# Row sums of the later modulation: transposed 32x32 blocks on VectorE instead of 512-column products on TensorE

## Chip, core and metric

The kernel runs on one core of a Trainium2 chip. The metric is the device time of one execution in microseconds (us). TensorE is PE in the profile (PEld are its weight loads), VectorE is DVE, ScalarE ACT, GpSimd POOL, and SyncE's transfer queue SPq.

## What is computed

A decoder trunk of two layers over 512 positions of width 2048: first differential attention, then forgetting attention on keys and values that are projected once from the stream after the first layer. Each layer shifts, scales and gates its input by vectors that come from one conditioning row c:

```python
c_act = silu(c)                                   # (1, 2048)
mod = c_act @ w_mod[l] + b_mod[l]                 # (1, 3 * 2048): shift, scale, gate
h = x * (1.0 + scale[:, None]) + shift[:, None]
y = mixer(h)                                      # attention of the layer
x = layer_norm(DN_ALPHA * x + gate[:, None] * y, ln_g[l], ln_b[l])
```

The shared keys and values have a shift and a scale of their own (`kv_w_mod`, `kv_b_mod`). So there are eight vectors of 2048 values, each a product of one row with a 2048x2048 matrix. The shift and scale of layer 0 are needed before anything else; this case is about the other six: gate of layer 0, shift and scale of the shared keys and values, shift, scale and gate of layer 1.

## The kernel before, in words

**The large products.** All weights come in as f32, two row blocks of 128 at a time (`WeightStream`, lines 50 to 106; tile wst), and are split into a rounded half whi (ScalarE, L93) and a remainder wlo (VectorE, L94). `group` (lines 306 to 348) runs one job of 512 columns: for each pair of row blocks and each of four accumulator banks a burst of six products, `products` (L173, L174, L175): high by high, high by low, low by high. After every burst it calls `tick`.

**What goes on beside them.** `tick` (line 290) takes the next entry of `pieces`, a list written out by hand with the steps of attention (score, turn, values, norm, store), and then advances the generator `background` as often as its argument bg says. The order in which the instructions of an engine end up is not only that of the code: a scheduler of the framework orders them by priority and readiness, so that ready work can stand earlier on its engine than the loop issues it. Between engines, waits follow from the tiles: a tile with bufs=1 can be written again only when its last reader is done.

**The later modulation.** `mod_stream` (lines 355 to 399) is that background. It works through segments of 512 columns. For each segment it loads the matrix's 16 row blocks (tile ms, or msk) and adds them up on VectorE, each row weighted by its value of c_act: one `tensor_scalar` (L389) and 15 `scalar_tensor_tensor` (L391) of 128x512 into the accumulator macc (two buffers). One tick is one of these 16 instructions. What is left is the sum over the 128 partitions. `mod_row` (lines 401 to 415) makes it, in two steps that run within the next segment, at its second and its sixth tick: first macc is split into mhi (ScalarE) and mlo (VectorE) by `split` (L168, L169; one buffer each) and the bias is loaded into mrow (L408); then two products with a 128x128 matrix of ones, 512 columns wide (L411, L412), give the row sum in the bank tr, VectorE adds the bias (L413, one partition, 512 values), and the row is stored to DRAM (L414).

There are two such streams. The first (lines 630 to 649) has four vectors, 16 segments: `gate_dram[0]`, both rows of `mod_dram[0]`, and the first row of `mod_dram[1]`. Its first tick is issued in the group qk[3], behind the first three heads' work; qk groups advance it in two bursts of three, vg groups in three of four, and what is left runs in `open_n` (line 913). The attention steps of heads 0 and 1 stand close together in `pieces`; from head 2 on they are spread out (`spread=True`). The second stream (lines 1090 to 1105) has two vectors, 8 segments (the second row of `mod_dram[1]` and `gate_dram[1]`), beside the projection of the shared values and keys (vj, kj). `fold` (line 931) reads `mod_dram[0]` back in `open_n` and `mod_dram[1]` during kj[2]; the gates are read in `out_projection` (line 884).

The bank tr (`tr_bank`, one buffer) is shared by these products and all transpositions on PE. Weights, ms, biases and rows all are issued in order on SyncE's queue.

Of the kernel before, what the change touches and what calls it, by code (L numbers as in the profile page):

```python
# [2 lines left out]

# [6 lines left out]
F32 = mybir.dt.float32  # L10
F32R = mybir.dt.float32r
I32 = mybir.dt.int32
AF = mybir.ActivationFunctionType
ALU = mybir.AluOpType

P = 128
D = 2048
# [92 lines left out]
def tile_yoco(  # L110
# [23 lines left out]
    nc = tc.nc  # L134
    V, S, PE, G = nc.vector, nc.scalar, nc.tensor, nc.gpsimd
# [6 lines left out]
    const = ctx.enter_context(tc.tile_pool(name="const", bufs=1))  # L142
# [12 lines left out]
    def acc_bank(name="acc"):  # L155
        return ps.tile([P, 512], F32, name=name, tag="acc", bufs=4)
# [4 lines left out]
    def tr_bank(name="tr"):  # L161
        return ps.tile([P, 512], F32, name=name, tag="tr", bufs=1)
# [4 lines left out]
    def split(hi, lo, src):  # L167
        S.copy(hi, src)  # L168
        V.tensor_tensor(lo, src, hi.bitcast(F32), op=ALU.subtract)  # L169
# [8 lines left out]
    ident = const.tile([P, P], F32, name="ident")  # L178
    make_identity(nc, ident)
    ones = const.tile([P, P], F32, name="ones")  # L180
    G.memset(ones, 1.0)
    mask = const.tile([P, 512], F32, name="mask")
    G.memset(mask, 0.0)
    G.affine_select(
# [14 lines left out]
    pt = tr_bank()  # L199
# [7 lines left out]
    pt = tr_bank()  # L207
# [147 lines left out]
    def mod_stream(segs, new_stage, new_acc, nk, deep=0, new_deep=None):  # L355

        todo = [(i, r) for i in range(len(segs)) for r in range(KT // nk)]
        loaded = {}  # L360
        summed = []

        def load(k):
            i, r = todo[k]
            src, col, _ = segs[i]
            t = new_deep() if k < deep else new_stage()
            rows = src[nk * r * P : nk * (r + 1) * P, col : col + 512]
            nc.sync.dma_start(t, rows.rearrange("(k p) n -> p k n", p=P) if nk > 1 else rows)
            loaded[k] = t

        def load_upto(k):
            n = len(loads)
            while n < len(todo) and n <= (k + 7 if n < deep else k + 2 // nk):
                load(n)
                loads.append(n)
                n += 1

        loads = []
        load_upto(-1)
        for k, (i, r) in enumerate(todo):  # L380
            load_upto(k)
            if r == 0:
                acc = new_acc()
            t = loaded.pop(k)
            for kk in range(nk):
                kt = nk * r + kk
                w = t[:, kk, :] if nk > 1 else t
                if kt == 0:
                    V.tensor_scalar(acc, w, cact[:, 0:1], None, op0=ALU.mult)  # L389
                else:  # L390
                    V.scalar_tensor_tensor(acc, w, cact[:, kt : kt + 1], acc, op0=ALU.mult, op1=ALU.add)  # L391
                if kt == KT - 1:
                    summed.append(segs[i][2](acc))
                if kt in (1, 5) and summed:
                    if next(summed[0], None) is None:
                        summed.pop()
                yield
        for _ in summed[0]:
            yield

    def mod_row(pool, ones_r, dst, bias, one):

        def steps(acc):
            hi = pool.tile([P, 512], F32R, name="mhi", tag="mhi", bufs=1)
            lo = pool.tile([P, 512], F32R, name="mlo", tag="mlo", bufs=1)
            split(hi, lo, acc)
            row = pool.tile([1, 512], F32, name="mrow", tag="mrow", bufs=1)
            nc.sync.dma_start(row, bias.rearrange("(o n) -> o n", o=1))  # L408
            yield True
            pt = tr_bank()  # L410
            PE.matmul(pt, ones_r, hi, start=True, stop=False)  # L411
            PE.matmul(pt, ones_r, lo, start=False, stop=True)  # L412
            V.scalar_tensor_tensor(row, pt[0:1, :], one, row, op0=ALU.add, op1=ALU.add)  # L413
            nc.sync.dma_start(dst, row)  # L414
        return steps


# [4 lines left out]
    with tc.tile_pool(name="start", bufs=2, reuse_waits="tile") as sp, tc.manual_schedule(engines={ET.DVE}):  # L422
# [44 lines left out]
        def mod_steps():  # L467
            for n, (i, k, nr) in enumerate(tiles):
                k0, nk = sets[i]
                load_mods(n + NBUF)  # L470
                if k >= KT - on_pe(i):
                    continue
                if k == 0:
                    accs[i] = sp.tile([P, 2, 2 * P], F32, name="sacc", tag="sacc", bufs=2)
                acc = accs[i][:, :, : nk * P]
                for kq in range(nr):
                    w, sc = loaded[i, k][:, kq, :, :], cact[:, k + kq : k + kq + 1]
                    if k + kq == 0:
                        V.tensor_scalar(acc, w, sc, None, op0=ALU.mult)
                    else:  # L480
                        V.scalar_tensor_tensor(acc, w, sc, acc, op0=ALU.mult, op1=ALU.add)  # L481
                    yield i
# [3 lines left out]
        steps = mod_steps()  # L486
# [46 lines left out]
        acc = {}  # L533
# [96 lines left out]
    actx = ExitStack()  # L630
    ap = actx.enter_context(tc.tile_pool(name="ap", bufs=1, reuse_waits="tile"))
    segs = []
    ones_a = ap.tile([P, P], F32R, name="ones_a")
    S.copy(ones_a, ones)
    for dst, src, col, bias, one in (
        (gate_dram[0], w_mod[0], 2 * D, b_mod[0], 0.0),
        (mod_dram[0][0:1, :], kv_w_mod, 0, kv_b_mod, 0.0),
        (mod_dram[0][1:2, :], kv_w_mod, D, kv_b_mod, 1.0),
        (mod_dram[1][0:1, :], w_mod[1], 0, b_mod[1], 0.0),
    ):  # L640
        for f0 in range(0, D, 512):
            cs = slice(col + f0, col + f0 + 512)
            segs.append((src, col + f0, mod_row(ap, ones_a, dst[:, f0 : f0 + 512], bias[cs], one)))
    background = mod_stream(
        segs,
        lambda: ap.tile([P, 2, 512], F32, name="ms", tag="ms", bufs=2),
# [342 lines left out]
    npool, n, nstats = zp  # L989
# [81 lines left out]
    acc = [acc_bank() for _ in range(TB)]  # L1071
    held = {}
    for i, (half, s) in enumerate(lag):
# [4 lines left out]
        hi, lo = held[s]  # L1078
# [8 lines left out]
            ws.advance(ws.where[id(vj[0]), s] + 4)  # L1087
    forget = [forget_logits(q) for q in range(4)] + [None, forget_sums] + [None] * 8 + [columns_of_f]
    pieces.extend(forget)
    ones_b = npool.tile([P, P], F32R, name="ones_b")  # L1090
    S.copy(ones_b, ones)
    segs = []
    for dst, col, one in ((mod_dram[1][1:2, :], D, 1.0), (gate_dram[1], 2 * D, 0.0)):
        for f0 in range(0, D, 512):
            cs = slice(col + f0, col + f0 + 512)
            segs.append((w_mod[1], col + f0, mod_row(npool, ones_b, dst[:, f0 : f0 + 512], b_mod[1, cs], one)))
    background = mod_stream(
        segs,
        lambda: npool.tile([P, 512], F32, name="ms", tag="ms", bufs=3),
# [236 lines left out]
```

## Time and profile before

| what | value |
|---|---|
| median of three runs | 2008.82 us (2008.1 to 2009.01) |
| the profiled execution | 2007.0 us |
| its span in the profile | 2005.2 us |
| mean granted clock of TensorE in it | 0.995 |
| L411 and L412, the products with ones | 24 each |

The profile is of one execution; its span goes from its first to its last instruction, and 1.8 us of that execution's 2007.0 us lie outside it. Times in a view are counted from the span's start. In groups of instructions, "x24 | 16.2, 675" means 24 of them, 16.2 us busy in all, 675 ns each on average; behind the next bar stands the idle time of the engine before them and what ended it. In lists in the order of time, each line begins with the start and the duration in us, and brackets give the idle time before it and its releaser. Matmuls are pipelined: a step begins before the last one has ended, so the distance of two starts says what one costs.

### The profile page before, as it was taken

The numbers are of one execution on the slowest core, as the hardware profiler recorded it, in microseconds if no ns is written. First come the engines' busy times: TensorE is split into PE (matmuls) and PEld (weight loads), VectorE is DVE, ScalarE is ACT, GpSimd is POOL, SyncE is SP. The second block draws the span as 40 slices with busy tenths as digits, with TensorE's granted clock in tenths as the row PEclk, the third lists the DMA queues.
The fourth block names the chain that finished last, engine by engine and source line by source line (L and its number), as shares of the span: only waits on it lengthen the run. The fifth ranks groups of instructions, "written<-read, shape, count | busy, mean of one in ns | idle before, by whom it ended". The sixth has DMA issues, their size and how long they took to land.

```text
span 2005.2 us, 25007 instructions
## 1 busy us (share of the span) xinstructions
PE 1964.4 (98%) x9115; PEld 1626.3 (81%) x9115; DVE 1336.4 (67%) x2435; ACT 725.0 (36%) x1234; POOL 2.2 (0%) x10
## 2 busy tenths in 40 slices
PE   5999999999999999999999999999999999999997
PEld 4888878888888888888878888888888888888885
DVE  7887865677777778853576666635455555576778
ACT  2422445333333334431263222224343334353132
POOL 0000000000000000000000000000000000000000
PEclk8999999999999999999999999999999999999999
DMA  9994742375757666453336687634323232333755
GB/s 343 347 315 145 243 151 85 106 230 185 225 178 231 189 223 213 158 166 100 121 137 223 234 276 260 225 95 129 103 90 105 95 102 93 96 120 97 257 190 175
DMA packets 263095, 353.79 MB, mean 176 GB/s; under 512 B 18022, under 2 KB 162556, under 8 KB 262204
## 3 DMA queue, kind: packets, MB, share of 16 engines
q1 hardware_dynamic: 260592, 347.99, 53.2%
q10 hardware_dynamic: 2380, 4.21, 0.6%
q8 instruction: 71, 1.16, 0.2%
q14 instruction: 52, 0.43, 0.1%
HBM read 339.47 MB, written 12.66 MB: 176 GB/s over the span
## 4 chain that ended last, share of the span: by engine, by line
PE 90%; DVE 4%; DMA 3%; SPq 1%; issue 1%; ACT 0%; DVEq 0%; ACTq 0%
PE acc L173 26%; PE acc L174 26%; PE acc L175 26%; DMA ms<-in_w_mod_dram 2%; PE sc L173 2%; PE sc L174 2%; PE sc L175 2%; PE o L175 1%; PE o L174 1%; PE o L173 1%; PE tr L1200 1%; DVE macc L391 1%; DVE wlo L94 1%; DMA sms<-in_w_mod_dram 1%; PE tr L727 0%
## 5 line engine op out<-in xcount | busy, mean ns | idle before, releaser
L94 DVE TENSOR_TENSOR wlo<-wst,whi 128x1024 fp32r<-128x1024 f32 (+2 forms) x339 | 404.7, 1196 | 278.3 <-ACT whi L93 266.8
L93 ACT CAST whi<-wst 128x1024 fp32r<-128x1024 f32 (+2 forms) x339 | 349.6, 1032 | 641.0 <-PE acc L175 323.0
L173 PE MATMUL acc<-whi,hh 128*128 128x512 f32 x1252 | 491.7, 396 | 0.9 <-ACT hh L967 0.8
L174 PE MATMUL acc<-wlo,hh 128*128 128x512 f32 x1252 | 489.1, 391 | 0.0
L175 PE MATMUL acc<-whi,hl 128*128 128x512 f32 x1252 | 488.2, 390 | 0.0
L173 PE MATMUL acc<-hh,whi 128*128 128x512 f32 x1184 | 470.4, 397 | 1.1 <-DVE sg L680 0.6
L175 PE MATMUL acc<-hh,wlo 128*128 128x512 f32 x1184 | 462.3, 390 | 0.0
L174 PE MATMUL acc<-hl,whi 128*128 128x512 f32 x1184 | 462.2, 390 | 0.0
L391 DVE SCALAR_TENSOR_TENSOR macc<-ms,cact,macc 128x512 f32<-128x512 f32 x300 | 225.0, 750 | 78.7 <-DMA ms<-in_w_mod_dram 53.8
L175 PEld LDWEIGHTS acc<-whi,hl 128*128 128x128 f32 x1252 | 235.3, 188 | 50.7 <-DVE hl L968 0.3
L173 PEld LDWEIGHTS acc<-whi,hh 128*128 128x128 f32 x1252 | 235.7, 188 | 48.5 <-ACT hh L967 1.2
L174 PEld LDWEIGHTS acc<-wlo,hh 128*128 128x128 f32 x1252 | 235.6, 188 | 46.4 <-DVE wlo L94 0.4
L175 PEld LDWEIGHTS acc<-hh,wlo 128*128 128x128 f32 x1184 | 222.3, 188 | 48.6
L173 PEld LDWEIGHTS acc<-hh,whi 128*128 128x128 f32 x1184 | 222.6, 188 | 43.8 <-PE acc L175 1.0
L174 PEld LDWEIGHTS acc<-hl,whi 128*128 128x128 f32 x1184 | 222.8, 188 | 39.3
L481 DVE SCALAR_TENSOR_TENSOR sacc<-sms,cact,sacc 128x512 f32<-128x512 f32 (+1 forms) x127 | 89.5, 705 | 5.2 <-DMA sms<-in_w_mod_dram 1.5
L710 ACT ACTIVATE e<-e,mn 128x128 f32<-128x128 f32 (+3 forms) x64 | 36.0, 563 | 126.2 <-DVE mn L706 126.0
L1189 ACT ACTIVATE eb<-eb,mnb 128x128 f32<-128x128 f32 (+1 forms) x64 | 36.1, 563 | 96.8 <-DVE mnb L1186 95.7
L1186 DVE CUSTOM_DVE_ANT_0 eb<-sc,biasb 128x128 f32<-128x128 f32 (+1 forms) x64 | 31.4, 490 | 52.7 <-PE sc L175 52.7
L391 DVE SCALAR_TENSOR_TENSOR macc<-msk,cact,macc 128x512 f32<-128x512 f32 x60 | 44.5, 750 | 14.5 <-DMA msk<-in_w_mod_dram 13.4
L1204 DVE TENSOR_TENSOR pTl<-tr,pTh 128x128 fp32r<-128x128 f32 (+1 forms) x64 | 31.2, 488 | 26.5 <-ACT pTh L1203 26.2
L706 DVE CUSTOM_DVE_ANT_0 e<-sc,bias 128x128 f32<-128x128 f32 (+3 forms) x64 | 31.1, 486 | 21.3 <-PE sc L175 21.2
(259 smaller groups left out, 1759.0 us busy)
## 6 DMA issues: line engine op xcount, KB each, us to landing
wst<-in_a_w_in_dram SPq DMA_DIRECT2D x240, 256.0 KB
ms<-in_w_mod_dram SPq DMA_DIRECT2D x64, 512.0 KB
ms<-in_kv_w_mod_dram SPq DMA_DIRECT2D x64, 512.0 KB
wst<-in_kv_w_dram SPq DMA_DIRECT2D x64, 512.0 KB
wst<-in_b_w_in_dram SPq DMA_DIRECT2D x128, 256.0 KB
sms<-in_w_mod_dram SPq DMA_DIRECT2D x56, 512.0 KB
wst<-in_b_w_out_dram SPq DMA_DIRECT2D x48, 512.0 KB
wst<-in_a_w_out_dram SPq DMA_DIRECT2D x32, 512.0 KB
```

Source lines behind the costliest of these rows:

```text
L93: self.nc.scalar.copy(hi[:, :, :w], st[:, :, :w])
L94: self.nc.vector.tensor_tensor(lo[:, :, :w], st[:, :, :w], hi[:, :, :w].bitcast(F32), op=ALU.subtract)
L173: PE.matmul(dst, lhs[0], rhs[0], start=start, stop=False)
L174: PE.matmul(dst, lhs[0], rhs[1], start=False, stop=False)
L175: PE.matmul(dst, lhs[1], rhs[0], start=False, stop=stop)
L391: V.scalar_tensor_tensor(acc, w, cact[:, kt : kt + 1], acc, op0=ALU.mult, op1=ALU.add)
L481: V.scalar_tensor_tensor(acc, w, sc, acc, op0=ALU.mult, op1=ALU.add)
L706: V.tensor_tensor_reduce(out=e[:, :w], in0=sc[:, :w], in1=st["bias"][:, (3 - i) * P :], scale=-1.0, scalar=3.0e38, op0=ALU.add, op1=ALU.mi ...
L710: S.activation(e[:, :w], e[:, :w], AF.Exp, bias=mn, scale=-1.0, accum_out=rs)
L1186: V.tensor_tensor_reduce(out=e[:, :w], in0=sc[:, :w], in1=bias[:, :w], scale=-1.0, scalar=3.0e38, op0=ALU.add, op1=ALU.min, accum_out=mn)
L1189: S.activation(e[:, :w], e[:, :w], AF.Exp, bias=mn, scale=-1.0, accum_out=rs)
L1204: V.tensor_tensor(pTl[:, 0 : i + 1, ts], src, pTh[:, 0 : i + 1, ts].bitcast(F32), op=ALU.subtract)
```

## The change

`mod_row`, once per segment, becomes `mod_rows`, once per vector of four segments. For each segment VectorE turns every 32x32 block of macc (`transpose`, tile mturn) and adds up each block's rows (`tensor_reduce` over 32 columns), which leaves 16 columns of 128 partial sums in mred (two buffers). When all four segments of a vector are there, 64 columns, one plain f32 product with `fours`, four 32x32 identities on top of each other, adds the four groups of partitions: 64 partitions by 32 columns of result. The bias and the store take that shape. `split`, mhi, mlo and the matrices of ones for it (ones_a, ones_b) are gone. The two steps still run at the second and the sixth tick of the next segment; the second does something only after a vector's fourth segment.

```diff
+    fours = const.tile([P, 32], F32, name="fours")
+    for k in range(0, P, 32):
+        G.tensor_copy(fours[k : k + 32, :], ident[k : k + 32, k : k + 32])
...
-    def mod_row(pool, ones_r, dst, bias, one):
-
-        def steps(acc):
-            hi = pool.tile([P, 512], F32R, name="mhi", tag="mhi", bufs=1)
-            lo = pool.tile([P, 512], F32R, name="mlo", tag="mlo", bufs=1)
-            split(hi, lo, acc)
-            row = pool.tile([1, 512], F32, name="mrow", tag="mrow", bufs=1)
-            nc.sync.dma_start(row, bias.rearrange("(o n) -> o n", o=1))
+    def mod_rows(pool, dst, bias, one):
+        red = []
+
+        def steps(n, acc):
+            if n == 0:
+                red.append(pool.tile([P, 64], F32, name="mred", tag="mred", bufs=2))
+            t = pool.tile([P, 512], F32, name="mturn", tag="mturn", bufs=1)
+            V.transpose(t, acc)
+            V.tensor_reduce(
+                red[0][:, 16 * n : 16 * n + 16], t.rearrange("p (j q) -> p j q", q=32), axis=mybir.AxisListType.X, op=ALU.add
+            )
+            if n == 3:
+                row = pool.tile([64, 32], F32, name="mrow", tag="mrow", bufs=1)
+                nc.sync.dma_start(row, bias.rearrange("(j q) -> j q", q=32))
             yield True
-            pt = tr_bank()
-            PE.matmul(pt, ones_r, hi, start=True, stop=False)
-            PE.matmul(pt, ones_r, lo, start=False, stop=True)
-            V.scalar_tensor_tensor(row, pt[0:1, :], one, row, op0=ALU.add, op1=ALU.add)
-            nc.sync.dma_start(dst, row)
+            if n == 3:
+                pt = tr_bank()
+                PE.matmul(pt[0:64, 0:32], red[0], fours, start=True, stop=True)
+                V.scalar_tensor_tensor(row, pt[0:64, 0:32], one, row, op0=ALU.add, op1=ALU.add)
+                nc.sync.dma_start(dst.rearrange("o (j q) -> (o j) q", q=32), row)
         return steps
...
-    ones_a = ap.tile([P, P], F32R, name="ones_a")
-    S.copy(ones_a, ones)
...
-        for f0 in range(0, D, 512):
-            cs = slice(col + f0, col + f0 + 512)
-            segs.append((src, col + f0, mod_row(ap, ones_a, dst[:, f0 : f0 + 512], bias[cs], one)))
+        steps = mod_rows(ap, dst, bias[col : col + D], one)
+        segs += [(src, col + 512 * f, partial(steps, f)) for f in range(4)]
```

The second stream is changed in the same way (`ones_b` goes, `mod_rows(npool, ...)` comes).

## Prediction

> **What bounds the kernel now.** I read the page first: its head, the slices of the granted clock, the chain that ended last.
>
> ```profile
> span 2005.2 us, 25007 instructions
> ...
> PE 1964.4 (98%) x9115; PEld 1626.3 (81%) x9115; DVE 1336.4 (67%) x2435; ACT 725.0 (36%) x1234; POOL 2.2 (0%) x10
> ...
> PEclk8999999999999999999999999999999999999999
> ...
> PE 90%; DVE 4%; DMA 3%; SPq 1%; issue 1%; ACT 0%; DVEq 0%; ACTq 0%
> ```
>
> PE has work nearly always, at full clock after the start, and nine tenths of the chain is PE. That is an average, so I cut the span into stretches (columns: stretch, length, busy time and instructions of each engine, clock, DMA).
>
> ```profile
> 176.00:280.00 104.00, 100.84 (x471) 82.66 (x470) 86.67 (x179) 42.60 (x90) 0.00 (x0) 1.00 0.66 212
> 280.00:400.00 120.00, 119.50 (x578) 99.56 (x577) 66.45 (x164) 51.59 (x108) 0.00 (x0) 1.00 0.31 97
> 400.00:500.00 100.00, 100.00 (x474) 83.20 (x474) 74.60 (x148) 35.34 (x70) 0.00 (x0) 1.00 0.64 205
> ...
> 700.00:730.00 30.00, 29.35 (x131) 23.92 (x131) 21.83 (x34) 8.47 (x17) 0.00 (x0) 1.00 0.69 223
> ...
> 1130.00:1250.00 120.00, 120.00 (x530) 99.29 (x529) 81.91 (x104) 30.77 (x37) 0.00 (x0) 1.00 0.79 263
> 1250.00:1360.00 110.00, 110.00 (x485) 90.69 (x484) 56.41 (x71) 31.35 (x38) 0.00 (x0) 1.00 0.49 159
> ```
>
> From 280 us to 1360 us, where the later modulation's products run, PE is filled, but for 0.65 us in 700:730 and 0.50 us in 280:400. Only in 176:280 does it lose more: 104.00 - 100.84 = 3.16 us, with DVE busy for 86.67 of 104 us. And the weights do not run short: ScalarE's splits wait for PE, not PE for them.
>
> ```profile
> ACT whi L93 <- PE acc L175: 323.0, 116, 9.4
> ```
>
> **What is removed from PE.** The 24 pairs of L411 and L412, in the order of time, one pair of the first background stream and the last of the second:
>
> ```profile
> 387.21 0.40 PE L411 MATMUL tr<-mhi,ones_a 128*128 128x512 f32 x1
> ...
> 387.44 0.40 PE L412 MATMUL tr<-mlo,ones_a 128*128 128x512 f32 x1
> ...
> 387.68 0.40 PE L173 MATMUL acc<-whi,hh 128*128 128x512 f32 x1
> ```
>
> ```profile
> 1355.72 0.40 PE L411 MATMUL tr<-mhi,ones_b 128*128 128x512 f32 x1
> ...
> 1356.19 0.39 PE L173 MATMUL acc<-hh,whi 128*128 128x512 f32 x1
> ```
>
> The 0.40 us is a latency; matmuls overlap. What a pair costs is the step from its start to the next instruction's: 387.68 - 387.21 = 0.47 us, and 1356.19 - 1355.72 = 0.47 us. So 24 x 0.47 = **11.3 us** leave PE, all between 387 us and 1356 us, where it is filled.
> The Trainium skill (TensorE: Matmul & The Clock Gate, section "Wait — 56ns, not 53.3ns?") gives the warm step as columns over 2.4 GHz plus about 2.5 ns, some 216 ns for 512 columns. By that rule, as an estimate, 48 x 0.216 = 10.4 us would leave; the steps here are 0.23 to 0.24 us, so the trace's are taken.
>
> **What is added to PE.** Six products, 64 columns of weights by 32 moving columns in plain f32. The trace has no such shape. The nearest rows are the eight 128x1 products of L511 and the 32x32 transposition of L934.
>
> ```profile
> 164.70 0.95 PE L511 MATMUL tr<-ones,sacc 128*128 128x1 f32 x8
> 165.51 0.49 PE L173 MATMUL sc<-hh,whi 128*128 128x512 f32 x1
> ```
>
> ```profile
> 879.18 0.39 PE L175 MATMUL acc<-whi,hl 128*128 128x512 f32 x1
> 879.50 0.24 PE L934 MATMUL tr<-ident,mrow 32*128 32x32 f32 x1
> ...
> 880.01 0.39 PE L174 MATMUL acc<-wlo,hh 128*128 128x512 f32 x1
> ```
>
> (165.51 - 164.70) / 8 = 0.10 us is the lower end. From 879.18 to 880.01 stand two 512-column products (0.46 us) and the transposition, so 0.37 us, a wait for its row included, is the upper end. I take 0.15 us, near L511, which is also a plain f32 product: 6 x 0.15 = **0.9 us** (0.6 to 2.2). PE's work falls by 11.3 - 0.9 = 10.4 us.
>
> **DVE, ACT, POOL and the queues.** Per segment of 512 columns DVE loses mlo (L169), and the row sum of L413 stays once per vector. It gains a turning copy and a reduction of 128x512; of those the trace shows neither. Nearest: the statistics of L901, which read 512 and write 6, the one-source L389, and L94 at 1024 elements.
>
> ```profile
> L413 DVE SCALAR_TENSOR_TENSOR mrow<-tr,mrow 1x512 f32<-1x512 f32 x24 | 16.2, 675 | 17.6 <-PE tr L412 15.3 <-DMA wst<-in_a_w_in_dram 2.4
> L169 DVE TENSOR_TENSOR mlo<-macc,mhi 128x512 fp32r<-128x512 f32 x24 | 16.2, 675 | 0.7 <-ACT mhi L168 0.7
> ...
> L901 DVE BATCH_NORM_STATS2 nstats<-n 128x6 f32<-128x512 f32 x16 | 10.5, 685 | 0.1
> ...
> L389 DVE TENSOR_SCALAR macc<-ms,cact 128x512 f32<-128x512 f32 x20 | 9.7, 483 | 5.0 <-DMA ms<-in_w_mod_dram 4.6
> ```
>
> ```profile
> L94 DVE TENSOR_TENSOR wlo<-wst,whi 128x1024 fp32r<-128x1024 f32 x315 | 384.4, 1221 | 277.8 <-ACT whi L93 266.3 <-DMA vld<-v_dram 8.4 <-DMA ms<-in_w_mod_dram 1.6
> ```
>
> Removed 24 x 1.35 = 32.4 us. Added: two instructions of 0.685 us per segment, 24 x 1.37 = 32.9 us, and six short sums over 64x32 at well under L389's 0.48 us, together 1 to 3 us. So DVE stands about where it was (+2 us). Ends: 0.48 and 1.22 us for each of the two, 24 x 0.96 = 23 us and 24 x 2.44 = 59 us, so -8 to +29 us. I take 0.685, the row with the same reading. PE hides either end from 400 us on, where DVE is busy for 74.60 of 100 us and +29 us over the thousand us of the two streams is 3%. Before that it counts, see the next part.
>
> ACT loses 24 casts of mhi, each of which waited its turn behind PE; nothing waits for ACT in the filled stretches, so 0. SP issues 6 + 6 small transfers in place of 24 + 24 (64 pieces of 128 bytes instead of one of 2 KB); the six stores in SP's queue wait for the product, and behind them wait weight loads, as behind 24 now: 0, and a gain if anything. POOL gets four 32x32 copies ahead of the mask:
>
> ```profile
> 1.94 0.29 POOL L184 TENSOR_SCALAR_AFFINE_SELECT mask<-mask 128x128 f32<-128x128 f32 x1
> 2.37 0.18 PEld L200 LDWEIGHTS tr<-ident,crow 16*128 16x128 f32 x1 [2.37 <-POOL mask L184]
> ...
> 4.01 0.18 DVE L206 TENSOR_TENSOR cact<-cact,ccol 128x16 f32<-128x16 f32 x1
> ...
> 5.70 0.35 DVE L479 TENSOR_SCALAR sacc<-sms,cact 128x256 f32<-128x256 f32 x1 [1.51 <-DMA sms<-in_w_mod_dram]
> ```
>
> Even if PE waited for them (4 x 0.29 = 1.2 us at L184's price), cact would be ready at 4.19 + 1.2 = 5.4 us, before the first weights land at 5.70: 0, at worst 1.2 us.
>
> **What the removal sets free.** The background's multiply-adds do not run where the loop places them. Rows of the accumulator macc in 20 us stretches, then the moment at 385 us, the end of the first group with ticks (qk[3]):
>
> ```profile
> 256.00:276.00 20.00, 7.51 (x10) 0.00 (x0) 1.00 0.59 190
> 276.00:296.00 20.00, 1.50 (x2) 0.00 (x0) 1.00 0.46 147
> 296.00:316.00 20.00, 0.00 (x0) 0.00 (x0) 1.00 0.27 86
> ...
> 376.00:396.00 20.00, 4.92 (x7) 0.62 (x1) 1.00 0.38 118
> ```
>
> ```profile
> 385.57 0.68 DVE L169 TENSOR_TENSOR k1l<-acc,k1h 128x512 fp32r<-128x512 f32 x1
> ...
> 387.64 0.62 ACT L168 CAST mhi<-macc 128x512 fp32r<-128x512 f32 x1 [2.77 <-PE tr L411]
> ...
> 389.19 0.49 DVE L389 TENSOR_SCALAR macc<-ms,cact 128x512 f32<-128x512 f32 x1
> ```
>
> Macs fill DVE up to 280 us, put ahead of the ticks that issue them, then stop until 389 us: the second segment's split needs the one mhi buffer, which PE's pair of the first frees at 387 us (tick 22, the first burst but one of vg[3]), and macc has two buffers. After the change nothing of a segment but the last of four touches PE, and mred has two buffers, so the pause from 280 to 387 us will fill with macs too. What that costs is seen in 176:280, above all here:
>
> ```profile
> 256.00:276.00 20.00, 17.79 (x89) 14.19 (x88) 18.26 (x43) 8.76 (x21) 0.00 (x0) 1.00 0.59 190
> ```
>
> ```profile
> 268.81 0.75 DVE L391 SCALAR_TENSOR_TENSOR macc<-ms,cact,macc 128x512 f32<-128x512 f32 x1 [0.62 <-DMA ms<-in_w_mod_dram]
> ```
>
> ```profile
> 274.20 0.41 PE L774 MATMUL tr<-ident,og 128*128 128x128 f32 x2 [0.85 <-DVE og L760]
> ```
>
> A mac at the head of DVE waits for its DMA, the attention's short steps queue behind it, and PE waits for them. 107 us at the rate of 176:280 lose 107 x 3.16 / 104 = 3.3 us, of which 0.5 us is lost today: **2.8 us** more. Ends: a gain of 0.65 us (no new loss, and the gap in 700:730 goes since the macs are done earlier) and, at the rate of 256:276 throughout, 107 x 2.21 / 20 = 11.8 us. I take the mean rate, as DVE would be about as full as in 176:280: (66.45 / 120) x 107 + (7.51 / 20) x 107 = 99 of 107 us.
>
> **Sum.** 11.3 - 0.9 - 2.8 = 7.6 us less. The profiled execution takes 2007.0 us, 1.8 us of it around the span; it would take 1999.4 us, span 1997.6 us. The median of the three runs shown lies 1.8 us above that execution: 2008.8 - 7.6 = **2001.2 us**.
>
> **The rivals.**
> *No new loss.* DVE finds its gaps and PE keeps all: 10.4 us, 1998.4 us. For it: 400:500 carries macs with PE at 100.00 of 100. Against: there attention is spread out in the list of pieces, for heads 0 and 1, up to about 337 us, it is not. 0.27.
> *The pause fills badly.* Half of it, 50 us of unspread attention, runs at the rate of 256:276 (5.5 us) and the other half at the mean rate (1.7 us), less the 0.5: 6.7 us lost, 2005.1 us, within 0.2% of before (4.0 us, about what a measurement of this kernel can tell). 0.10.
> *PE's time isn't the bound.* A profile's busy PE contains latency, so the products may lie in gaps and 2008.8 us stays. Against: 188 ns of weight load (from PEld 99.29 us over 529) in each 0.23 us step leave no gap for another, and the starts quoted follow back to back. 0.06.
> The Trainium skill (Perfetto Trace Analysis, section "Identifying the Most-Contended Engine") speaks for this rival: busy time of matmuls misleads, weight-load share is to be read. That share is 81% here, which looks like slack, but 188 of 230 ns is 82%, a filled PE.
> *Slower: the macs run ahead all the way.* With no product to hold them, DVE keeps meeting DMA waits in front of attention steps for the whole first stream. At 176:280's rate, 0.030 us per us, that costs 10.4 us as soon as it lasts 342 us past 280 us; up to 878 us it costs 18.2 us: 2008.8 - 10.4 + 18.2 = 2016.6 us, also what a turning copy at 1.22 us would push towards. Against: from 400 us on macs already run as densely, without loss. 0.14.
>
> **How the numbers follow.** The forecast (1999.5 to 2003.5 us) has 0.43. Faster by over 0.2%: 0.43 + 0.27 = 0.70; within: 0.16; slower: 0.14. The range: below, 11.3 - 0.6 + 0.65 = 11.35 us, 1997.5 us; above, 2009.5 us, past the case without gain; the slower rival stays outside.
>
> **What would show it.** PE's count falls by 42 and no product of 512 columns into tr is left; the product takes 0.10 to 0.37 us; turning copy and reduction near 0.685 us each. Macs fill 296:376, and PE's busy share there falls to about 97%. The second stream's stretch (884 to 1360 us) stays filled and becomes 8 x 0.47 - 2 x 0.15 = 3.5 us shorter. Wrong if macs still pause at 296 us, if PE opens gaps past 400 us, or if the copy takes over 1 us.

## The result, and the profile after

| | before | after |
|---|---|---|
| median | 2008.91 us (2007.82 to 2013.49, 6 runs) | 2023.7 us (2022.11 to 2026.71, 6 runs) |
| ratio, 95% interval | | 1.0074 [1.0063, 1.0084] |
| profiled execution | 2007.0 us, span 2005.2 us | 2022.11 us, span 2020.3 us |

The change is 0.74% slower, 14.8 us, where 7.6 us less were forecast. The head and the shares of the chain on the page of after:

```profile
span 2020.3 us, 24855 instructions
...
PE 1962.2 (97%) x9079; PEld 1619.1 (80%) x9079; DVE 1336.6 (66%) x2441; ACT 707.6 (35%) x1208; POOL 2.9 (0%) x14
...
PE 72%; DVE 12%; DMA 12%; issue 2%; SPq 1%; ACT 1%; DVEq 0%; ACTq 0%
```

PE has 36 instructions fewer (48 products gone, 12 added: each of the six vector products runs as two), and hardly less busy time. DVE's busy time is the same to 0.2 us. What changed is the chain: PE has 72% of it instead of 90%, DVE and DMA together 24% instead of 7%. The same stretches as before (length, then PE, PEld, DVE, ACT, POOL, clock, DMA):

```profile
176.00:280.00 104.00, 101.03 (x471) 82.70 (x470) 88.13 (x181) 40.61 (x85) 0.00 (x0) 1.00 0.68 213
280.00:400.00 120.00, 115.81 (x554) 95.53 (x553) 105.77 (x233) 49.42 (x109) 0.00 (x0) 1.00 0.72 225
400.00:500.00 100.00, 94.70 (x437) 78.20 (x436) 79.28 (x154) 31.25 (x64) 0.00 (x0) 0.98 0.73 230
500.00:600.00 100.00, 95.57 (x441) 77.62 (x440) 81.25 (x158) 32.63 (x66) 0.00 (x0) 1.00 0.72 229
...
1130.00:1250.00 120.00, 120.00 (x531) 98.96 (x530) 81.30 (x103) 29.95 (x34) 0.00 (x0) 1.00 0.82 272
1250.00:1360.00 110.00, 109.40 (x477) 88.82 (x476) 55.12 (x69) 27.59 (x33) 0.00 (x0) 1.00 0.56 182
```

Three stretches that PE had filled (but for 0.5 us) are open now: 4.2, 5.3 and 4.4 us between 280 and 600 us, and DVE is busy for 105.77 of 120 us in the first. The rows with the accumulator macc in 20 us stretches, and then at 700 us (a second table of the same view):

```profile
276.00:296.00 20.00, 8.84 (x14) 1.00 0.77 246
296.00:316.00 20.00, 10.54 (x15) 1.00 0.81 255
...
700.00:800.00 100.00, 0.00 (x0) 1.00 0.27 85
```

The pause is filled, as forecast. But the multiply-adds (macs below) do not settle into the old pace after it: in the stretch 700 to 800 us none is left. The same row of before:

```profile
700.00:800.00 100.00, 35.73 (x49) 1.86 (x3) 1.00 0.66 213
```

Of these 49 instructions of DVE 46 are macs. In after the first stream's last mac starts at 678 us, in before at 832 us. What that does is seen in DVE's list at the boundary of two groups, and in PE's:

```profile
434.14 1.22 DVE L95 TENSOR_TENSOR wlo<-wst,whi 128x1024 fp32r<-128x1024 f32 x1
437.17 1.54 DVE L396 SCALAR_TENSOR_TENSOR macc<-ms,cact,macc 128x512 f32<-128x512 f32 x2 [1.81 <-DMA ms<-in_kv_w_mod_dram]
439.73 1.54 DVE L396 SCALAR_TENSOR_TENSOR macc<-ms,cact,macc 128x512 f32<-128x512 f32 x2 [1.02 <-DMA ms<-in_kv_w_mod_dram]
441.19 1.22 DVE L95 TENSOR_TENSOR wlo<-wst,whi 128x1024 fp32r<-128x1024 f32 x1
442.32 0.42 DVE L170 TENSOR_TENSOR vl<-acc,vh 128x256 fp32r<-128x256 f32 x1
442.66 0.74 DVE L396 SCALAR_TENSOR_TENSOR macc<-ms,cact,macc 128x512 f32<-128x512 f32 x1
443.31 0.41 DVE L691 SCALAR_TENSOR_TENSOR sg<-th,acc 128x256 f32<-128x256 f32 x1
```

```profile
439.40 0.39 PE L176 MATMUL acc<-whi,hl 128*128 128x512 f32 x1
443.87 0.77 PE L174 MATMUL acc<-hh,whi 128*128 128x512 f32 x1 [4.09 <-DVE sg L691]
444.44 0.63 PE L175 MATMUL acc<-hl,whi 128*128 128x512 f32 x1
444.86 0.63 PE L176 MATMUL acc<-hh,wlo 128*128 128x512 f32 x1
```

PE has ended a group and needs the accumulator bank emptied by vl and sg. Ahead of these on DVE stand macs that wait 1.81 and 1.02 us for row blocks still on their way. PE stands for 4.09 us. Gaps of this kind (for sg, for the attention's og and e, for q0l, and one of 0.82 us at 509 us for the new mrow, which stands on DVE behind macs that wait 1.53 us) add up to 17.2 us between 276 and 620 us, by the distances of PE's starts beyond the step of a matmul; in before it is 0.65 us.

The distance of the n-th accumulating product of after from that of before, as **lag**, tells where the time went (it is counted from the starts in PE's list, at before's times): +4.1 us at 179 us, +4.0 at 276, +7.9 at 365, +13.6 at 448, +20.3 at 659, then down to +16.1 at 876 and +14.9 at 1382. So there are two losses, one before 179 us and one from 276 to 660 us, and after that PE gains, as forecast: from 659 to 876 us 7 pairs x 0.47 = 3.3 us and before's gap of 0.65 us at 728 us, less 0.44 us for one new product, are 3.5 us, where 4.2 are seen.

### The profile page after: what moved, and what is told of

Its sections match the earlier page's. It is cut to its first block, busy times and chain, and to the rows that moved or that the text cites. A ratio compares the mean times of both kernels' runs of the same rounds, so it can differ in the third digit from the quotient of the medians.

```text
span 2020.3 us, 24855 instructions
## 1 busy us (share of the span) xinstructions
PE 1962.2 (97%) x9079; PEld 1619.1 (80%) x9079; DVE 1336.6 (66%) x2441; ACT 707.6 (35%) x1208; POOL 2.9 (0%) x14
## 4 chain that ended last, share of the span: by engine, by line
PE 72%; DVE 12%; DMA 12%; issue 2%; SPq 1%; ACT 1%; DVEq 0%; ACTq 0%
PE acc L174 21%; PE acc L176 21%; PE acc L175 21%; DMA ms<-in_kv_w_mod_dram 5%; DMA ms<-in_w_mod_dram 4%; DVE macc L396 4%; DVE wlo L95 3%; PE sc L174 1%; PE sc L176 1%; PE sc L175 1%; PE o L176 1%; PE o L175 1%; PE o L174 1%; PE tr L1208 1%; DMA sms<-in_w_mod_dram 1%
## 5 line engine op out<-in xcount | busy, mean ns | idle before, releaser
L1211 ACT CAST pTh<-tr 128x128 fp32r<-128x128 f32 (+1 forms) x64 | 27.2, 425 | 43.5 <-PE tr L1208 42.4
```

Source lines behind the costliest of these rows:

```text
L1211: S.copy(pTh[:, 0 : i + 1, ts], src)
```

## The experiments

Three theories were named before the runs. A: the pair of products had held the macs back, through the one mhi buffer, and it is their running ahead that costs. B: the new instructions themselves cost it (copy, reduction, product). C: the tile `fours`, made at the start, costs the first 4 us.

**Holding the first mac of each segment in program order.**

```diff
-                    V.tensor_scalar(acc, w, cact[:, 0:1], None, op0=ALU.mult)
+                    tc.keep_in_program_order(V.tensor_scalar(acc, w, cact[:, 0:1], None, op0=ALU.mult))
```

> The changed kernel, with one thing more: the first multiply of each segment (L394) is kept behind everything that the program has issued to VectorE before it, so that no segment starts ahead of its tick; the product per vector stays. Theory A (the removed pair of products had held the multiply-adds back; set free, they and their DMA waits stand in front of attention's steps and of the bank evacuations on VectorE): the eleven gaps of PE between 276 and 620 us, 17.2 us in all, nearly vanish, no macc instruction runs before about 330 us, and the time comes to 2000 to 2007 us. Theory B (the new instructions themselves cost it: turning copy, reduction, product, the wait for the bias sum): the gaps stay and so does the time, 2020 to 2025 us. Theory C (the four copies and the shift of the tiles behind them slow the start by 4.4 us): the start stays 4 us late under either.

Measured: 2028.43 us, ratio 1.0092 [1.0078, 1.0105], outside the range of either theory. The early gaps go, and others open late (the table of stretches of this kernel, then its rows with macc, then PE's list):

```profile
176.00:280.00 104.00, 104.00 (x490) 86.06 (x489) 58.47 (x134) 43.52 (x90) 0.00 (x0) 1.00 0.33 102
```

```profile
176.00:280.00 104.00, 0.00 (x0) 1.00 0.33 102
```

```profile
872.73 0.41 PE L785 MATMUL tr<-ident,og 128*128 128x128 f32 x2 [2.27 <-DVE og L771]
```

Without macs in 176:280, PE is filled there, and the lag falls from +6.3 us at 179 to +2.3 at 276: the 3.16 us that before loses there come from macs too. But the loop order is no better place for them. They now stand in order before the evacuations at every boundary (3.33 us at 438), and those left over run until 898 us (before: 832). PE waits for them there, 2.84 us for mred at 900 us among others, and the lag goes from +12.1 us at 850 to +23.0 at 890. Theory A in its simple form, that any hold brings the time back, is refuted; the place of each mac matters.

**One buffer for mred.**

```diff
-                red.append(pool.tile([P, 64], F32, name="mred", tag="mred", bufs=2))
+                red.append(pool.tile([P, 64], F32, name="mred", tag="mred", bufs=1))
```

> The changed kernel with one buffer of mred instead of two: the second vector's first reduction must wait for the first vector's product, which PE reaches near 490 us, so that macs can run ahead by some six segments and then pause. Theory A: the gaps before about 380 us stay (5.7 us), those between 380 and 490 us go (5 to 6 us), later ones stay in part: 2013 to 2019 us, with a pause of the macs before 490 us in the trace. Theory B: 2020 to 2025 us. Theory C says nothing of it.

Measured: 2023.31 us, 1.0078 [1.0064, 1.0092], no different from after: theory A's 2013 to 2019 us did not come, and the time alone would fit B. The macs pause for a hundred microseconds, and there PE is filled (stretches, then rows with macc):

```profile
400.00:500.00 100.00, 100.00 (x471) 83.29 (x470) 41.82 (x96) 35.50 (x69) 0.00 (x0) 1.00 0.30 96
```

```profile
400.00:500.00 100.00, 0.32 (x1) 1.00 0.30 96
```

The gaps before 400 us stay and others come later (1.84 us at 542, 3.43 us at 743): the loss moved. A hold at every fourth segment is too coarse.

**The tile `fours` alone, and later.** First, before with the tile and its four copies, read by nobody:

```diff
+    fours = const.tile([P, 32], F32, name="fours")
+    for k in range(0, P, 32):
+        G.tensor_copy(fours[k : k + 32, :], ident[k : k + 32, k : k + 32])
```

> The kernel before with nothing but the tile fours and its four copies on GpSimd added (it is not read): what the start pays for them. Theory C: the stretch up to 180 us is 4 us longer, 2012 to 2014 us. Theories A and B, with the 4.4 us being chance of that execution's transfers: 2008 to 2010 us.

Measured: 2012.87 us, 1.0021 [1.0012, 1.0029]: 4.4 us, theory C's size. Then after with the tile made by ACT in each stream's own pool, when the start is over:

```diff
+    def new_fours(pool):
+        t = pool.tile([P, 32], F32, name="fours")
+        for k in range(0, P, 32):
+            S.copy(t[k : k + 32, :], ident[k : k + 32, k : k + 32])
+        return t
```

> The changed kernel with fours built by ScalarE when the start is over, one tile in each stream's pool, instead of on GpSimd at the very beginning. Theory C: the start is back to that of before, 2018 to 2020 us. Theories A and B: 2021 to 2026 us, with macs ahead and gaps as in the changed kernel.

Measured: 2023.68 us, 1.0062 [1.005, 1.0075]. In the profiled execution the lag at 179 us is +0.7 instead of +4.1 us, and 17.5 us of gaps from 276 to 700 us stay. By the ratios only 0.0012 is won back from after, and the intervals overlap; so the start's loss is shown by before with `fours` and in the trace, not by this time. The second stream gains 3.0 us (13.8 to 10.8), the 8 x 0.47 - 2 x 0.44 = 2.9 us of its products.

**Less work on PE with the hold kept.** Before with both products cut to the first 32 of 512 columns (the other 480 sums are left out), so that mhi is still freed by PE; VectorE's sum behind them is cut to 32 columns too, 0.18 instead of 0.68 us each:

```diff
-            PE.matmul(pt, ones_r, hi, start=True, stop=False)
-            PE.matmul(pt, ones_r, lo, start=False, stop=True)
-            V.scalar_tensor_tensor(row, pt[0:1, :], one, row, op0=ALU.add, op1=ALU.add)
+            PE.matmul(pt[:, 0:32], ones_r, hi[:, 0:32], start=True, stop=False)
+            PE.matmul(pt[:, 0:32], ones_r, lo[:, 0:32], start=False, stop=True)
+            V.scalar_tensor_tensor(row[:, 0:32], pt[0:1, 0:32], one, row[:, 0:32], op0=ALU.add, op1=ALU.add)
```

> The kernel before, with the two products of each segment cut to 32 of their 512 columns, all tiles, splits and waits as they were (the sums of the other 480 columns are left out). It takes PE's work away and keeps the hold on mhi and mlo. If PE's time is the bound where these products run: 48 x about 0.17 us = 8 us less, 1999 to 2002 us. If the products lie in gaps: 2007 to 2010 us. Theories A and B both expect the first.

Measured: 2005.48 us, 0.9981 [0.9972, 0.999], 3.3 us faster, against 1999 to 2002 us expected. A short pair still takes 0.23 us, so 24 x 0.24 = 5.8 us left PE. In the first stream they are seen: the lag goes from +1.8 us at 276 to -3.2 at 914. Then 1.9 us are lost near 1025 us, where the granted clock is 0.68 and 0.50 in 1022:1024 and 1024:1026 (in before 1.00 in 1018:1028), and three waits for wlo between 1237 and 1268 us give 2.2 us back. PE's time is a bound, but not all of it comes out at the end. That VectorE also had 24 x 0.5 = 12 us less to do was not separated.

**The hold alone.** Before with all its work, but the pair reads a column of ones in place of mhi and mlo (the row sums become constants), so that nothing on PE frees mhi any more:

```diff
-            PE.matmul(pt, ones_r, hi, start=True, stop=False)
-            PE.matmul(pt, ones_r, lo, start=False, stop=True)
+            other = ones_r[:, 0:1].broadcast_to([P, 512])
+            PE.matmul(pt, ones_r, other, start=True, stop=False)
+            PE.matmul(pt, ones_r, other, start=False, stop=True)
```

> The kernel before, with the two products of each segment reading a constant in place of mhi and mlo (the rows' sums are left out; splits, products, their number and their size stay). mhi is free again as soon as mlo is made, so the multiply-adds lose what held them and nothing else changes. Theory A: macs in the pause from 280 to 387 us, gaps of PE up to 620 us of 8 to 15 us in all, 2015 to 2022 us. Theory B: no new instruction, so 2007 to 2010 us.

Measured: 2032.8 us, 1.0124 [1.0111, 1.0138]: **24.0 us slower, with no new instruction and none less on PE**. Theory A had put it at 2015 to 2022 us, B at 2007 to 2010. The rows with macc, DVE's list and PE's at the same boundary:

```profile
280.00:340.00 60.00, 26.71 (x39) 1.86 (x3) 1.00 0.71 227
...
700.00:800.00 100.00, 0.00 (x0) 0.00 (x0) 1.00 0.26 85
```

```profile
439.57 0.42 DVE L169 TENSOR_TENSOR vl<-acc,vh 128x256 fp32r<-128x256 f32 x1
443.01 0.75 DVE L391 SCALAR_TENSOR_TENSOR macc<-ms,cact,macc 128x512 f32<-128x512 f32 x1 [3.02 <-DMA ms<-in_kv_w_mod_dram]
443.68 0.41 DVE L681 SCALAR_TENSOR_TENSOR sg<-th,acc 128x256 f32<-128x256 f32 x1
```

```profile
444.24 0.77 PE L173 MATMUL acc<-hh,whi 128*128 128x512 f32 x1 [4.04 <-DVE sg L681]
```

The pause fills, the macs end early, and one of them stands for 3.02 us between vl and sg, as in after. The lag is +2.5 us at 276, +26.6 at 659, and +25 from 740 us to the end. This refutes B as the main cause and shows A's core: the hold was worth more than the products cost. The loss is larger than after's in part because the pair itself suffers: it and the transpositions share the bank tr, and PE stands 1.48 us (469 us) and 3.21 us (582 us) in front of a pair until VectorE has read al out of tr, and 0.38 and 1.98 us until it has read mrow.

**The change with a hold of the old pace.** The late-`fours` version, and for every segment a 32-column copy of macc into a one-buffer tile that a small product on PE frees at the sixth tick:

```diff
+            held = pool.tile([P, 32], F32R, name="mheld", tag="mheld", bufs=1)
+            S.copy(held, acc[:, 0:32])
...
+            pt = tr_bank()
+            PE.matmul(pt[0:32, 0:32], held, held, start=True, stop=True)
```

> The changed kernel with fours built after the start, and with a hold like that of before: per segment ScalarE copies 32 columns of macc into a one-buffer tile, and a product of 32 by 32 on PE at the segment's sixth tick reads it, so that macs can run ahead no further than they could. Theory A: the gaps between 276 and 620 us go, 1999 to 2005 us, under both kernels. Theory B: the turning copy and the reduction are still there, 2014 to 2022 us.

Measured: 2009.03 us, 0.9999 [0.999, 1.0008]: level with before, and well below the late-`fours` version without the hold (1.0062). It lies 4 us above theory A's range and 5 below B's. Stretches, and rows with macc:

```profile
280.00:400.00 120.00, 119.51 (x581) 99.54 (x580) 66.04 (x163) 50.55 (x108) 0.00 (x0) 1.00 0.32 101
400.00:500.00 100.00, 98.84 (x465) 81.31 (x464) 75.43 (x148) 34.08 (x70) 0.00 (x0) 1.00 0.65 202
```

```profile
280.00:340.00 60.00, 0.00 (x0) 0.00 (x0) 1.00 0.27 88
400.00:500.00 100.00, 35.05 (x48) 0.65 (x3) 1.00 0.65 202
```

The pause is back, and with it the time. The rows of PE's list of this kernel give the price of a held product:

```profile
386.44 0.40 PE L176 MATMUL acc<-whi,hl 128*128 128x512 f32 x1
386.67 0.18 PE L423 MATMUL tr<-mheld 128*32 128x32 f32 x1
386.70 0.47 PE L174 MATMUL acc<-whi,hh 128*128 128x512 f32 x1
387.01 0.39 PE L175 MATMUL acc<-wlo,hh 128*128 128x512 f32 x1
```

387.01 - 386.44 less two steps of 0.23 is 0.11 us, so PE has 11.3 - 6 x 0.44 - 24 x 0.11 = 6.0 us less to do than before; gaps of 9.2 us from 276 to 1400 us against before's 3.2 take these up (0.98 us at 435, 1.57 at 727, several waits for wlo around 1250 us).

**What in `fours` costs the start.** Before with an unread tile of the same 128 bytes per partition at its place, set once and never copied to:

```diff
+    pad = const.tile([P, 32], F32, name="pad")
...
+    G.memset(pad, 0.0)
```

> The kernel before with an unread tile of 128 bytes per partition at the place of fours, and one memset instead of the four copies. If theory C's 4.4 us come from the shift of all tiles behind it: 2012 to 2014 us, with the transfers of 20 to 60 us at about 345 GB/s. If they come from GpSimd's copies at the start: 2007 to 2009.5 us, at about 383 GB/s.

And the same with `[P, 128]`, 512 bytes:

> The kernel before with the unread tile of 32 f32 per partition (128 bytes, 2013.0 us) made 128 f32 per partition (512 bytes). If what costs 4 us at the start is where later tiles begin within a row of 512 bytes, the shift by a whole 512 changes nothing: 2008 to 2009.5 us, with 383 GB/s between 20 and 60 us as before. If any shift or any lost room costs it: 2013 us, with 345 GB/s there.

Measured: 2012.97 us, 1.0026 [1.0016, 1.0035] with 128 bytes; 2007.82 us, 1.0003 [0.9994, 1.0012] with 512. The stretch from 20 to 60 us (GB/s last) of before, after, the 128-byte and the 512-byte version:

```profile
20.00:60.00 40.00, 35.24 (x165) 28.95 (x164) 34.89 (x53) 12.24 (x18) 0.00 (x0) 0.87 1.09 383
```

```profile
20.00:60.00 40.00, 32.52 (x146) 26.27 (x146) 32.45 (x49) 10.48 (x16) 0.00 (x0) 0.87 1.11 345
```

```profile
20.00:60.00 40.00, 32.45 (x137) 26.05 (x136) 32.06 (x48) 8.62 (x14) 0.00 (x0) 0.83 1.11 345
```

```profile
20.00:60.00 40.00, 35.00 (x164) 28.66 (x164) 34.61 (x52) 11.90 (x18) 0.00 (x0) 0.87 1.09 383
```

Not the copies: a tile that moves all later tiles by 128 bytes takes the loads from 383 to 345 GB/s, and one that moves them by 512 bytes takes nothing. So it is where the tiles behind it, those of the loads among them, begin in a row of SBUF, the memory of the tiles. The Trainium skill (DMA: Bandwidth & Descriptors, section "How a descriptor splits into AXI transactions") says that where a descriptor doesn't begin at a multiple of 256 bytes, its first transaction begins at the 256-byte boundary below, and the bytes ahead of the start are fetched unused and still cost beats. The runs agree in direction, 345 against 383 GB/s; but here it is the destination that moved, and that it is this, and not some other effect of the address, they do not show.

**The hold in the first stream alone.** The held version, with copy and product left out of the second stream:

```diff
+            if hold:
+                held = pool.tile([P, 32], F32R, name="mheld", tag="mheld", bufs=1)
+                S.copy(held, acc[:, 0:32])
```

> The version with late fours and one held 32-column product per segment (2009.0 us), with the held copy and product in the first stream alone; the second stream (8 segments) is as in the changed kernel. Theory A (the removed pair had held back the macs, and only the first stream, beside attention, needs that): the second stream keeps its whole gain, 8 x 0.47 - 2 x 0.44 = 2.9 us, as it did where fours came late without any hold (lag 13.8 to 10.8 us), instead of losing 2.0 us as it did with the hold (lag -0.7 to +1.3 us): about 4.9 us less than 2009.0, so 2004 us (2002 to 2006), 0.2% faster than before. Rival (the second stream's gain goes to late weights between 1230 and 1300 us whatever holds the macs, as in the kernel with short products): 8 held products of 0.11 us go and nothing else, 2008 us, no difference from before.

Measured: 2008.61 us, 1.0005 [0.9996, 1.0014]: the rival's number, not theory A's 2004 us. DVE's list, and PE's waits from 1200 to 1300 us:

```profile
1220.88 2.37 DVE L392 SCALAR_TENSOR_TENSOR macc<-ms,cact,macc 128x512 f32<-128x512 f32 x3 [0.69 <-DMA ms<-in_w_mod_dram]
1227.28 0.75 DVE L392 SCALAR_TENSOR_TENSOR macc<-ms,cact,macc 128x512 f32<-128x512 f32 x1 [4.03 <-DMA ms<-in_w_mod_dram]
1227.95 1.22 DVE L95 TENSOR_TENSOR wlo<-wst,whi 128x1024 fp32r<-128x1024 f32 x1
```

```profile
PE acc L176 <- DVE wlo L95: 2.6, 5, 1.1
```

Here too a mac waits for its DMA with wlo, which PE needs, behind it. Before shows such waits at that place (3.21 us at 1223) without a gap on PE.

**One buffer more for the row blocks of the second stream.** In the version above, and as a control in before (`head_rows`, which uses the same buffers, takes 4 too):

```diff
-        lambda: npool.tile([P, 512], F32, name="ms", tag="ms", bufs=3),
+        lambda: npool.tile([P, 512], F32, name="ms", tag="ms", bufs=4),
```

> The version with the hold in the first stream alone (2008.6 us) with four instead of three buffers for the row blocks ms of the second stream, so that each is loaded one step earlier. Theory (between 1200 and 1300 us a multiply-add that waits up to 4.0 us for its row block stands at the head of VectorE and holds up the weights' remainders behind it, for which TensorE waits 3.6 us in all): the waits shrink, the gaps go, and the second stream keeps its 2.9 us; 2004 to 2005.5 us. Rival (the row blocks and weights come at the rate that the transfers allow, 0.71 to 0.84 of their time being busy there, and another buffer changes only where the wait is seen): 2008 to 2009 us.

> The kernel before with four instead of three buffers for ms of the second stream. There TensorE has no gap between 1100 and 1340 us, so by both theories it is the same as before: 2007.5 to 2009 us. It is the control of the version above: what it gains is not owed to the changed row sums.

Measured: 2006.7 us, 0.9997 [0.9989, 1.0006], and 2006.69 us, 0.9994 [0.9985, 1.0002]. In the first, PE's wait for wlo in 1200:1300 falls (its waits):

```profile
PE acc L176 <- DVE wlo L95: 0.7, 2, 0.4
```

From 914 to 1382 us the lag changes by -1.1 us instead of +1.9. So the mechanism is right in the trace, but the time lies between the two ranges, and the whole is no faster than before by more than its interval, nor than the control. No version with the changed row sums beat the kernel before; only the short products did, which leave work out.

## Why the prediction was wrong

1. *PE is the bound, and 11.3 us leave it*: right in size, and where nothing takes them they come out: 3.5 us due and 4.2 seen from 659 to 876 us, 2.9 and 3.0 in the second stream of the late-`fours` version. In after the second stream gives 1.1 us (16.05 to 14.94), where the prediction had 3.5. Of the missing 2.4 us, 0.9 are waits for wlo around 1270 us and 0.6 the larger products of step 2; the rest was not placed.

2. *The product, 0.15 us (0.10 to 0.37)*: too small. PE's list of after:

```profile
506.07 0.40 PE L176 MATMUL acc<-whi,hl 128*128 128x512 f32 x1
506.40 0.30 PE L426 MATMUL tr<-fours,mred 128*64 128x32 f32 x2
506.63 0.50 PE L174 MATMUL acc<-whi,hh 128*128 128x512 f32 x1
506.97 0.40 PE L175 MATMUL acc<-wlo,hh 128*128 128x512 f32 x1
```

506.97 - 506.07 less two steps of 0.23 is 0.44 us, nearly a pair's 0.47. Six make 2.6 instead of 0.9 us, so 8.7 and not 10.4 us left PE.

3. *Copy and reduction, 0.685 us each, hidden*: right (groups of after, mean ns behind the busy time):

```profile
L416 DVE STREAM_TRANSPOSE mturn<-macc 128x512 f32<-128x512 f32 x24 | 17.0, 707 | 0.4
L417 DVE TENSOR_REDUCE mred<-mturn 128x16 f32<-128x512 f32 x24 | 16.3, 678 | 0.2
```

4. *The four POOL copies, "0, at worst 1.2 us"*: failed. The copies cost nothing, but the tile they fill costs 4.2 to 4.4 us by shifting the others. The step priced instructions and not addresses.

5. *"What the removal sets free", 2.8 us*: this is the step that failed most. It saw that mhi's one buffer made the pause and that the pause would fill, and up to 387 us it was near: the lag rises by 4.1 us there. But it let the cost end at 387 us; its ground, named with the rivals, was that 400:500 carries macs with PE at 100.00 of 100. That row was taken under the hold: the macs there were paced by PE's pairs. Once free, they ran ahead until the last at 678 us, and from 387 to 659 us the lag rises by another 12.2 us, although eight pairs are gone there. In all 17.2 us of gaps opened where 0.65 had been. The rival *the macs run ahead all the way* had the mechanism, at 0.14; its argument "Against" was that same row. It put the loss at 0.030 us per us over 598 us, 18.2 us; it was (17.2 - 0.65) / 344 = 0.048 over the 344 us from 276 to 620 us. That 18.2 and 16.5 us lie so near is luck: the rate was too low and the time too long. Its 2016.6 us lacks steps 2 and 4: 2016.6 + 1.7 + 4.2 = 2022.5 us. The range, too, was narrower than the prediction's own ends: 2008.8 - 11.3 + 2.2 + 11.8 - 0.5 = 2011.0 us, not 2009.5.

The sum of the profiled executions: 4.1 (start) + 16.5 (gaps) + 0.9 (wlo) - 8.7 (PE) = 12.8 of 15.1 us. The other 2.3 us were not placed one by one; the slower steps after two long gaps, below, can make up to 3.4 us. That the macs' running ahead is the main cause is shown by the hold taken alone (+24.0 us) and put back (level with before, with `fours` made late; 1.0062 without the hold). Why the scheduler places a free mac ahead of sg was not tried.

## What to carry to other kernels

Before removing work from the bounding engine, ask which buffers it frees: a product that costs 0.47 us can be the pacemaker of a background whose running ahead costs more. A row that shows "no loss" under a hold says nothing about the time without it. And a new small constant can shift the addresses of what is allocated after it: here 128 bytes ahead of the first loads' tiles cost 4 us; 512 bytes, or the same tile in a later pool, left the loads at 383 GB/s.

## What was not expected of the hardware

- A shift of SBUF tiles by 128 bytes lowered the loads at the start from 383 to 345 GB/s; by 512 bytes it did not.
- The plain f32 product of 32 columns ran as two instructions and took 0.44 us of PE's time, while one 32-column product on rounded operands (fp32r) took 0.11 us. The number of passes alone does not make it: the short pair, two products of 32 columns on fp32r, took 0.23 us. Whether it is the type or what goes with it was not separated.
- After long gaps PE's steps were longer: 444.86 - 444.44 = 0.42 us instead of 0.23 behind the 4.09 us. The granted clock (the third number from the end) of after around that gap:

```profile
436.00:456.00 20.00, 15.91 (x66) 12.86 (x65) 15.99 (x27) 4.95 (x12) 0.00 (x0) 0.91 0.80 253
```

And behind one of 2.53 us for q0l that ended at 599.76 us:

```profile
602.00:604.00 2.00, 2.00 (x10) 1.90 (x10) 1.99 (x3) 0.00 (x0) 0.00 (x0) 0.50 0.67 201
```

The second drop came when PE had been at work again for about one microsecond: the first longer step is that from 600.79 to 601.14 us. In after's trace each of the two drops lasts 3.4 us (mean 0.51 in 443.8:447.2 and in 600.8:604.2), and so costs PE up to 1.7 us. In the profiles of this case between 70 and 1980 us, each of the twelve gaps of PE of 2.1 us or more had such a drop around its end; of seven gaps from 1.5 to 2.0 us one had. But the two gaps of 0.80 and 0.84 us ahead of the drop near 1025 us in the short-product run were enough there, and about the same two in before (0.52 and 0.84 us) were not. A long wait on DVE so costs PE twice: the wait, and some microseconds at half the clock.
